# Half of a blocked fp32 projection through Strassen's seven products, on one Trainium2 core

## The chip, the cores and the metric

The kernel runs on one core of a Trainium2 chip. The metric is the device time of one execution in microseconds. Three runs of the kernel before gave a median of 1344.21 us (1343.96 to 1344.87).

## What is computed

A decoder block with 256 tokens and a model width of 2048: one combined input projection (2048 x 9216), attention and a gated MLP as token mixers, an output projection, a layer norm, and then the feed-forward part, which the change touches:

```
h = layer_norm(ALPHA * x + mix)
a = square(relu(h @ w_ff1 + b_ff1))      # 2048 -> 8192
y = layer_norm(ALPHA * h + a @ w_ff2 + b_ff2)   # 8192 -> 2048
```

Everything is fp32. The kernel splits every factor of a matrix product into a high part (the factor rounded to fp32r) and a low part (the rest), and adds the three products high x high, high x low and low x high.

## The kernel before

**Chunks, pieces, steps.** All weights pass through one pipeline. A chunk is 512 rows by 512 columns of a weight matrix (1 MB), loaded by SP's queue into one of three raw tiles (`issue_load`, L128). A piece is half a chunk: 256 rows, so two contraction tiles of 128 rows, by 512 columns. `emit_splits` (L152) takes a tile from a ring of six and makes the piece's high part on ScalarE (L171), and `emit_low` (L140) makes its low part on VectorE (L142). After the low part of a chunk's last piece the load of the third chunk after it is issued (L144). A step (`run_step`, L183) is TensorE's work with one piece; when it is done, the piece's tile goes back to the ring. So in step s the split of piece s + 5 is written into the program, and it waits until TensorE has finished step s - 1. The order of the steps is the order of the groups in the code, and each engine takes its instructions in the order in which the main loop (L766 to L780) writes them: the splits of the step, then deferred work (`rounds`, `later`), then the matmuls, then the evacuation of a group's accumulators.

**The feed-forward part** is cut into eight blocks of 1024 hidden columns. Block b has two groups of the first projection (`ff1`, 8 pieces each) and four groups of the last projection (`ff2`, one for each 512 output columns, 4 pieces each). The program runs the first projection of block b and then the last projection of block b - 1.

- A piece of `ff1` ("F" below) keeps the weights stationary: for each of 4 output tiles and 2 contraction tiles one matmul of 512 columns (the high weights times the high and low activations, L219) and one of 256 (the low weights times the high activations, L221). The four accumulators of the group come from a pool of six PSUM banks. Its evacuation is `halves` (L237): ScalarE copies one half of the bank with the bias (L242), VectorE adds the other (L244). Later steps square it (L535) and split it into high and low (`hilo`, L89 to L91).
- A piece of `ff2` ("E" below) keeps activations stationary: for each of 2 token tiles and 2 contraction tiles the three products of 512 columns (L207 to L209). The groups end with one addition of 128 x 512 per token tile into the residual y (L553).

**The end.** The last block's `ff2` groups run in an order by token tiles, with extra tiles (`LATE`, L544) beside the ring, and the second layer norm follows. Its gain and bias are loaded as wide tiles in blocks 2 and 3 (L703).

Of the kernel before, what the change touches and what calls it, by code (L numbers as in the profile page):

```python
# [11 lines left out]
F32 = mybir.dt.float32  # L12
F32R = mybir.dt.float32r
I32 = mybir.dt.int32
AF = mybir.ActivationFunctionType
ALU = mybir.AluOpType
AX = mybir.AxisListType

P = 128
S = 256  # L20
NT = S // P
# [7 lines left out]
CW = 512  # L29
# [3 lines left out]
RING = tuple(f"R{i}" for i in range(6))  # L33
LOOK = len(RING) - 1
NCT = CW // P
WARM = (256, 256, 256, 128)
EARLY = 3
NBUCKET = 32
# [30 lines left out]
def block_kernel(ctx: ExitStack, tc: tile.TileContext, xT, x, w_in, rel_bias, lnv_g, lnv_b, wsT, b_sp,  # L69
# [36 lines left out]
    def add_pieces(g, sizes=None, cs=None):  # L106
        out = []
        for c in cs or range(g.nk // KC):
            r0 = g.row + c * KC * P
            chunks.append(g.src[r0:r0 + KC * P, g.col:g.col + CW].rearrange("(k p) n -> p k n", p=P))  # L110
            k0 = 0
            for n in (sizes or {}).get(c, (KH,) * (KC // KH)):
                out.append(len(pieces))
                pieces.append(dict(g=g, chunk=len(chunks) - 1, k0=k0, k=c * KC + k0, n=n, last=k0 + n == KC, uses=0))
                k0 += n
        return out

    def add_step(piece, part, first=False, last=False):
        pieces[piece]["uses"] += 1
        steps.append((piece, part, first, last))  # L120
        return len(steps) - 1

    def add_group(g, sizes=None):
        hs = add_pieces(g, sizes)
        for h in hs:
            add_step(h, "all", h == hs[0], h == hs[-1])
# [10 lines left out]

    lows = []

    def emit_low(h):  # L140
        sl = raw_t[h["chunk"]][:, h["k0"]:h["k0"] + h["n"], :]
        nc.vector.tensor_tensor(h["lo"], sl, f32(h["hi"]), op=ALU.subtract)  # L142
        if h["last"]:
            issue_load(h["chunk"] + NRAW)  # L144
            for f in load_post.pop(h["chunk"], []):
                f()
# [5 lines left out]
    def emit_splits():  # L152


        while state["split"] < len(pieces):
            h = pieces[state["split"]]
            early = h["g"].early
            if lows and early is None:
                return
            tags = h["g"].tags  # L160
            tag = next((t for t in free if t in tags), None) or next((t for t in free if t in RING), None)
            if tag is None:
                return
            free.remove(tag)
            if h["chunk"] in split_with:
                split_with[h["chunk"]](h["k0"], h["n"])
            n = h["n"]
            t = big.tile([P, 2, KH, CW], F32R, name="w2", tag=tag)
            h["tag"], h["hi"], h["lo"] = tag, t[:, 0, :n, :], t[:, 1, :n, :]
            sl = raw_t[h["chunk"]][:, h["k0"]:h["k0"] + n, :]  # L170
            nc.scalar.activation(h["hi"], sl, AF.Copy)  # L171
            state["split"] += 1
            if early is not None and h["k"] >= early * KH:
                lows.append(h)
            else:
                emit_low(h)
# [6 lines left out]
    def run_step(s):  # L183
        piece, part, first, last = steps[s]
        h = pieces[piece]
        g, n, k0 = h["g"], h["n"], h["k"]
        hi, lo = h["hi"], h["lo"]
        if g.mode == "as":

            toks = range(NT) if part == "all" else [part]  # L190
            if n == 1:

                ps_ = [bank(g, i) for i in toks]
                av = g.act(k0)
                a = [[av[:, e * S + i * P:e * S + (i + 1) * P] for e in range(2)] for i in toks]
                for i in toks:
                    nc.tensor.matmul(ps_[i], a[i][0], hi[:, 0], start=first, stop=False)
                    nc.tensor.matmul(ps_[i], a[i][1], hi[:, 0], start=False, stop=False)
                for i in toks:
                    nc.tensor.matmul(ps_[i], a[i][0], lo[:, 0], start=False, stop=False)  # L200
            for i in toks if n > 1 else ():
                t, cs = (i[0], slice(i[1] * S, (i[1] + 1) * S)) if isinstance(i, tuple) else (i, slice(0, CW))
                p = bank(g, i)[:, cs]
                for kk in range(n):
                    av = g.act(k0 + kk)
                    ah, al = av[:, t * P:(t + 1) * P], av[:, S + t * P:S + (t + 1) * P]
                    nc.tensor.matmul(p, ah, hi[:, kk, cs], start=first and kk == 0, stop=False)  # L207
                    nc.tensor.matmul(p, ah, lo[:, kk, cs], start=False, stop=False)  # L208
                    nc.tensor.matmul(p, al, hi[:, kk, cs], start=False, stop=last and kk == n - 1)  # L209
        else:  # L210
            toks = {"lo01": (0, 1), "lo23": (2, 3)}.get(part, range(NCT))
            for ot in toks:
                p = bank(g, ot)
                ws_ = slice(ot * P, (ot + 1) * P)
                for kk in range(n):
                    av = g.act(k0 + kk)
                    st, en = first and kk == 0, last and kk == n - 1
                    if part == "all":
                        nc.tensor.matmul(p, hi[:, kk, ws_], av, start=st, stop=False)  # L219
                    if part in ("all", "lo01", "lo23"):  # L220
                        nc.tensor.matmul(p[:, :S], lo[:, kk, ws_], av[:, :S], start=False, stop=en)  # L221
                    if part in (0, 1):
                        ts = slice(part * P, (part + 1) * P)
                        nc.tensor.matmul(p.rearrange("p (a t) -> p a t", a=2)[:, :, ts], hi[:, kk, ws_],  # L224
                                         av.rearrange("p (a t) -> p a t", a=2)[:, :, ts], start=st, stop=False)
        h["uses"] -= 1
        if h["uses"] == 0:
            free.append(h["tag"])
        if last:
            for i in toks:  # L230
                g.evac(i, g.p.pop(i))
            if g.after and not g.p:
                g.after()

    later, rounds = [], []

    def halves(p, bias=None):  # L237
        t = work.tile([P, S], F32, name="half", tag="half", bufs=3)
# [276 lines left out]
    def load_wide(key, src, tag):  # L515
        tiles[key] = big.tile([P, D], F32, name="wide", tag=tag)
        nc.sync.dma_start(tiles[key], bcast(src, D))

    def residual2(c, part):
# [4 lines left out]
        else:  # L524
            y = tiles["y", part - 1][:, sl]
            nc.vector.scalar_tensor_tensor(y, y, ALPHA, tiles["ln1_g"][:, sl], op0=ALU.mult, op1=ALU.mult)
            nc.vector.tensor_tensor(y, y, bb, op=ALU.add)

    def ev_ff1(f):
        def fin(ot, s):  # L530
            if ot == 0:
                tiles["a", f] = big.tile([P, NCT, 2 * S], F32R, name="a", tag=f"A{f % 4}")
            a = tiles["a", f]
            q = work.tile([P, S], F32, name="sq", tag="sum", bufs=7)
            nc.vector.scalar_tensor_tensor(q, s, 0.0, s, op0=ALU.max, op1=ALU.mult)  # L535
            rounds.append((hilo, a[:, ot, :S], a[:, ot, S:], q))

        def ev(ot, p):
            k = f * NCT + ot
            later.append((fin, ot, halves(p, bff1[:, k:k + 1])))  # L540
        return ev

    NB = FF // 1024
    LATE = ("A4", "A5", "W", "S10", "S11", "S12")  # L544

    def ev_ff2(blk, c):
        def ev(i, p):
# [67 lines left out]
    def quad(key):  # L615
        return lambda k: tiles[key][k // 4][:, k % 4, :]
# [5 lines left out]
    def at(s, f, *a):  # L622
        side.setdefault(s, []).append((f, a))
# [55 lines left out]
    for part in (0, 1, "lo01", "lo23"):  # L679
        for h in hs:  # L680
            s = add_step(h, part, part == 0 and h == hs[0], part not in (0, 1) and h == hs[-1])

    def ff1(f):
        add_group(Group(w_ff1, f * CW, 16, quad("hT"), "ws", ev_ff1(f), tags=wide if f == 1 else ()))

    def ff2(blk, c):
        return Group(w_ff2, c * CW, 8, lambda k: tiles["a", 2 * blk + k // NCT][:, k % NCT, :], "as",
                     ev_ff2(blk, c), row=blk * 1024, tags=LATE if blk == NB - 1 else ())

# [4 lines left out]
            at(s + 13 + 3 * i + j, residual2, i, j)  # L694
    for b in range(1, NB):
        j = len(chunks)
        ff1(2 * b)
        ff1(2 * b + 1)
        if b == 1:
            for i, a in enumerate((("ln1_b", ln1_b, "S11"), ("b_ff2", b_ff2, "S10"), ("ln1_g", ln1_g, "S12"))):  # L700
                load_post[j + 2 * i] = [lambda a=a: load_wide(*a)]
        elif b < 4:
            load_post[j] = [lambda a=(("ln2_b", ln2_b, "S6"), ("ln2_g", ln2_g, "S13"))[b - 2]: load_wide(*a)]  # L703
        if b == NB - 1:
            at(len(steps), free.extend, LATE[:3])
        for c in range(4):
            add_group(ff2(b - 1, c))
    add_group(ff2(NB - 1, 0))
    hss = [add_pieces(ff2(NB - 1, c)) for c in range(1, 4)]
    for part, hs in ((0, hss[0]), (0, hss[1]), (0, hss[2]), (1, hss[0]), (1, hss[1]), ((1, 0), hss[2]), ((1, 1), hss[2])):  # L710
# [104 lines left out]
```

## Time and profile before

| | |
|---|---|
| median of 3 runs | 1344.21 us |
| the profiled execution | 1344.47 us, of which its span is 1342.8 us |
| TensorE matmuls busy | 1331.8 us, 99% of the span, 6916 matmuls |
| VectorE busy | 831.7 us, 62% |
| ScalarE busy | 625.8 us, 47% |
| GpSimd busy | 5.1 us |
| DMA | 259.46 MB, 193 GB/s |

The profile is of one execution. The span goes from its first to its last instruction. Busy times are sums over an engine's instructions without overlaps. Matmuls overlap in the array, so a matmul's own duration is longer than the distance to the next one: it is the distance that counts for the time.

### The profile page before, as it was taken

The numbers are of one execution on the slowest core, as the hardware profiler recorded it, in microseconds if no ns is written. First come the engines' busy times: TensorE is split into PE (matmuls) and PEld (weight loads), VectorE is DVE, ScalarE is ACT, GpSimd is POOL, SyncE is SP. The second block draws the span as 40 slices with busy tenths as digits, with TensorE's granted clock in tenths as the row PEclk, the third lists the DMA queues.
The fourth block names the chain that finished last, engine by engine and source line by source line (L and its number), as shares of the span: only waits on it lengthen the run. The fifth ranks groups of instructions, "written<-read, shape, count | busy, mean of one in ns | idle before, by whom it ended". The sixth has DMA issues, their size and how long they took to land.

```text
span 1342.8 us, 17128 instructions
## 1 busy us (share of the span) xinstructions
PE 1331.8 (99%) x6916; PEld 1126.9 (84%) x6916; DVE 831.7 (62%) x1183; ACT 625.8 (47%) x832; POOL 5.1 (0%) x15
## 2 busy tenths in 40 slices
PE   8999999999999999999999999999999999999997
PEld 6888888888888888889888888888888888888886
DVE  6554677564545787568669565565565655655666
ACT  4444465454545555345554443443544434435531
POOL 0000000000000000000000000000000000000000
PEclk9999999999999999999999999999999999999999
DMA  9766445555555567553865656656555555565541
GB/s 324 277 193 218 158 157 169 181 183 189 188 189 187 176 199 254 180 196 116 287 224 188 219 188 213 194 184 187 189 185 190 188 183 190 184 186 190 187 174 63
DMA packets 128800, 259.46 MB, mean 193 GB/s; under 512 B 4808, under 2 KB 7376, under 8 KB 127824
## 3 DMA queue, kind: packets, MB, share of 16 engines
q1 hardware_dynamic: 127984, 254.94, 57.9%
q0 software_dynamic: 592, 3.16, 0.7%
q8 instruction: 54, 0.88, 0.3%
q10 hardware_dynamic: 144, 0.26, 0.1%
q14 instruction: 26, 0.21, 0.0%
HBM read 256.23 MB, written 2.11 MB: 192 GB/s over the span
## 4 chain that ended last, share of the span: by engine, by line
PE 97%; DMA 1%; DVE 1%; ACT 0%; issue 0%; SPq 0%; DVEq 0%
PE mm L219 36%; PE mm L221 19%; PE mm L208 13%; PE mm L209 13%; PE mm L207 13%; PE mm L224 1%; DVE w L142 1%; DMA raw<-in_w_in_dram 1%; DMA raw<-in_w_ff_dram 0%; DMA xraw<-in_xT_dram 0%; PE aux L387 0%; PE aux L495 0%; PE aux L295 0%; PE aux L325 0%; PE aux L317 0%
## 5 line engine op out<-in xcount | busy, mean ns | idle before, releaser
L142 DVE TENSOR_TENSOR w<-raw,w 128x1024 fp32r<-128x1024 f32 (+1 forms) x466 | 565.6, 1219 | 459.4 <-ACT w L171 459.3
L171 ACT ACTIVATE w<-raw 128x1024 fp32r<-128x1024 f32 (+1 forms) x466 | 489.6, 1055 | 603.3 <-PE mm L221 335.6
L219 PE MATMUL mm<-hT,w 128*128 128x512 f32 x960 | 336.6, 393 | 0.8 <-DVE sum L244 0.8
L219 PE MATMUL mm<-xs,w 128*128 128x512 f32 x896 | 315.7, 395 | 0.0
L221 PE MATMUL mm<-hT,w 128*128 128x256 f32 x1024 | 275.7, 279 | 0.0
L221 PE MATMUL mm<-xs,w 128*128 128x256 f32 x896 | 250.0, 279 | 0.0
L219 PEld LDWEIGHTS mm<-hT,w 128*128 128x128 f32 x960 | 179.9, 187 | 44.0 <-DVE sum L244 1.1
L209 PE MATMUL mm<-w,a 128*128 128x512 f32 (+1 forms) x520 | 204.1, 392 | 0.0
L207 PE MATMUL mm<-w,a 128*128 128x512 f32 (+1 forms) x520 | 204.1, 392 | 0.0
L208 PE MATMUL mm<-w,a 128*128 128x512 f32 (+1 forms) x520 | 204.1, 392 | 0.0
L219 PEld LDWEIGHTS mm<-xs,w 128*128 128x128 f32 x896 | 167.9, 187 | 39.7
L221 PEld LDWEIGHTS mm<-hT,w 128*128 128x128 f32 x1024 | 187.7, 188 | 0.3
L221 PEld LDWEIGHTS mm<-xs,w 128*128 128x128 f32 x896 | 168.0, 187 | 0.2
L207 PEld LDWEIGHTS mm<-w,a 128*128 128x128 f32 x520 | 97.9, 188 | 23.0
L209 PEld LDWEIGHTS mm<-w,a 128*128 128x128 f32 x520 | 97.9, 188 | 22.9
L208 PEld LDWEIGHTS mm<-w,a 128*128 128x128 f32 x520 | 97.9, 188 | 22.7
L207 PE MATMUL mm<-w,merged 128*128 128x512 f32 x128 | 50.9, 398 | 0.0
L209 PE MATMUL mm<-w,merged 128*128 128x512 f32 x128 | 50.7, 396 | 0.0
L208 PE MATMUL mm<-w,merged 128*128 128x512 f32 x128 | 50.7, 396 | 0.0
L207 PE MATMUL mm<-w,xs 128*128 128x512 f32 x120 | 49.5, 412 | 1.0 <-ACT w L171 1.0
L244 DVE TENSOR_TENSOR sum<-mm,half 128x256 f32<-128x256 f32 x136 | 49.0, 417 | 0.0
L208 PE MATMUL mm<-w,xs 128*128 128x512 f32 x120 | 47.7, 397 | 1.3 <-DVE w L142 1.3
(142 smaller groups left out, 970.7 us busy)
## 6 DMA issues: line engine op xcount, KB each, us to landing
raw<-in_w_ff_dram SPq DMA_DIRECT2D x128, 1024.0 KB, 5.2
raw<-in_w_in_dram SPq DMA_DIRECT2D x68, 1024.0 KB, 5.1
raw<-in_w_out_dram SPq DMA_DIRECT2D x16, 1024.0 KB, 5.1
raw<-in_w_pa_dram SPq DMA_DIRECT2D x8, 1024.0 KB, 5.1
raw<-in_w_pb_dram SPq DMA_DIRECT2D x8, 1024.0 KB, 5.1
raw<-in_w_in_dram SPq DMA_DIRECT2D x6, 512.0 KB, 8.0
y<-in_x_dram POOLq DMA_DIRECT2D x2, 1024.0 KB, 6.3
wide<-in_ln_b_dram SPq DMA_DIRECT2D x2, 1024.0 KB, 8.4
```

The lines of the kernel that those rows point to most:

```text
L142: nc.vector.tensor_tensor(h["lo"], sl, f32(h["hi"]), op=ALU.subtract)
L171: nc.scalar.activation(h["hi"], sl, AF.Copy)
L207: nc.tensor.matmul(p, ah, hi[:, kk, cs], start=first and kk == 0, stop=False)
L208: nc.tensor.matmul(p, ah, lo[:, kk, cs], start=False, stop=False)
L209: nc.tensor.matmul(p, al, hi[:, kk, cs], start=False, stop=last and kk == n - 1)
L219: nc.tensor.matmul(p, hi[:, kk, ws_], av, start=st, stop=False)
L221: nc.tensor.matmul(p[:, :S], lo[:, kk, ws_], av[:, :S], start=False, stop=en)
L224: nc.tensor.matmul(p.rearrange("p (a t) -> p a t", a=2)[:, :, ts], hi[:, kk, ws_], av.rearrange("p (a t) -> p a t", a=2)[:, :, ts], start= ...
L244: nc.vector.tensor_tensor(s, p[:, :S], t, op=ALU.add)
```

## The change

In blocks 1 to 6 the output columns 0 to 1023 of the last projection are no longer computed as 8 products of (128 tokens x 512) times (512 x 512), but as 7 (Strassen's scheme; the code names them P1 to P7). The columns 1024 to 2047 stay as they were.

- **Weights.** P3 and P2 use a chunk of the weights as it is and go through the raw tiles. The five others take their weights from two held tiles of 1 MB (tags S10 and S11). GpSimd's queue loads them, and adds further weight blocks to them by DMAs with `accum_op=add`. Tile 0 is used by P1, then one block is added, P5, another block, P6, a third block, P4. Tile 1 is a load and an addition, for P7. So each block has two plain loads and four adding ones on GpSimd's queue. An addition is issued after the low part of the last piece that used the tile's former value.
- **Activations.** VectorE makes four sums of 128 x 128 for each of four column tiles (`sum_of_acts`), and ScalarE and VectorE split them into high and low, after the second `ff1` group of a block.
- **Steps.** A piece of a product is used for one 128-token tile only: 6 matmuls of 512 columns. Products accumulate in the two banks of the small PSUM pool. P1, P5, P6 and P7 are added up over the six blocks in a tile `acc` (in the first block copied there by ScalarE), P3, P2 and P4 in y. At the end `collect` combines them with 8 additions of 128 x 512.
- **Order.** The 38 steps of a section follow `ORDER`: 16 F of the next block, 14 pieces of products and 8 E. `mixed` writes it out, for sections 2 to 7.
- The wide loads of the second layer norm's gain and bias move to the start of the last block's `ff2`, and so do the extra tiles of `LATE`.

```diff
+ORDER = ("F F F P1 F P1 F F F P5 F P5 F F F P6 F P6 F P3 P3 F P7 F P7 F "
+         "E P2 E P2 E E P4 E P4 E E E").split()
...
+    def add_held(g, key, done=None):
+        out = []
+        for k0 in range(0, KC, KH):
+            out.append(len(pieces))
+            pieces.append(dict(g=g, chunk=None, held=key, done=done, k0=k0, k=k0, n=KH, last=k0 + KH == KC, uses=0))
+        return out
...
+    def source(h):
+        t = tiles[h["held"]] if h["chunk"] is None else raw_t[h["chunk"]]
+        return t[:, h["k0"]:h["k0"] + h["n"], :]
     def emit_low(h):
-        sl = raw_t[h["chunk"]][:, h["k0"]:h["k0"] + h["n"], :]
+        sl = source(h)
         nc.vector.tensor_tensor(h["lo"], sl, f32(h["hi"]), op=ALU.subtract)
-        if h["last"]:
+        if h["last"] and h["chunk"] is None:
+            if h["done"]:
+                h["done"]()
+        elif h["last"]:
             issue_load(h["chunk"] + NRAW)
             for f in load_post.pop(h["chunk"], []):
                 f()
...
-            sl = raw_t[h["chunk"]][:, h["k0"]:h["k0"] + n, :]
-            nc.scalar.activation(h["hi"], sl, AF.Copy)
+            nc.scalar.activation(h["hi"], source(h), AF.Copy)
...
+        if g.mode == "sum":
+            if first:
+                sums["p"] = psx.tile([P, CW], F32, name="aux")
+            p = sums["p"]
+            for kk in range(n):
+                ah, al = g.act(k0 + kk)
+                nc.tensor.matmul(p, ah, hi[:, kk], start=first and kk == 0, stop=False)
+                nc.tensor.matmul(p, ah, lo[:, kk], start=False, stop=False)
+                nc.tensor.matmul(p, al, hi[:, kk], start=False, stop=last and kk == n - 1)
+            h["uses"] -= 1
+            if h["uses"] == 0:
+                free.append(h["tag"])
+            if last:
+                g.evac(p)
+            return
...
+    later, rounds, sums = [], [], {}
...
+    def sum_of_acts(f, ot, q):
+        if f % 2 == 0:
+            return
+        if ot == 0:
+            for i in range(2):
+                tiles["ca", i] = big.tile([P, 2, NCT, 2, P], F32R, name="ca", tag=("S6", "S13")[i])
+        q0, t0, t1 = tiles["q", ot], slice(0, P), slice(P, S)
+        cb = work.tile([P, 4, P], F32, name="cb", tag="pt")
+        nc.vector.tensor_tensor(cb[:, 0], q0[:, t1], q[:, t1], op=ALU.subtract)
+        nc.vector.tensor_tensor(cb[:, 2], q0[:, t0], q0[:, t1], op=ALU.subtract)
+        nc.vector.tensor_tensor(cb[:, 1], cb[:, 0], q0[:, t0], op=ALU.subtract)
+        nc.vector.tensor_tensor(cb[:, 3], q[:, t0], cb[:, 1], op=ALU.add)
+        for i in range(2):
+            d = tiles["ca", i][:, :, ot]
+            rounds.append((hilo, d[:, :, 0], d[:, :, 1], cb[:, 2 * i:2 * i + 2]))
...
+            summed = f // 2 in SUMMED
+            if summed and f % 2 == 0:
+                q = tiles["q", ot] = work.tile([P, S], F32, name="q0", tag="es"[ot // 2])
+            else:
+                q = work.tile([P, S], F32, name="sq", tag="sum", bufs=7)
             nc.vector.scalar_tensor_tensor(q, s, 0.0, s, op0=ALU.max, op1=ALU.mult)
             rounds.append((hilo, a[:, ot, :S], a[:, ot, S:], q))
+            if summed:
+                sum_of_acts(f, ot, q)
...
-    LATE = ("A4", "A5", "W", "S10", "S11", "S12")
+    SUMMED = range(1, NB - 1)
+    def held_load(blk, i):
+        def block(r, c):
+            r0 = blk * 1024 + r * CW
+            return w_ff2[r0:r0 + CW, c * CW:(c + 1) * CW].rearrange("(k p) n -> p k n", p=P)
+        tiles["b", i] = big.tile([P, KC, CW], F32, name="held", tag=("S10", "S11")[i])
+        nc.gpsimd.dma_start(tiles["b", i], block(0, i))
+        if i == 1:
+            nc.gpsimd.dma_start(tiles["b", 1], block(1, 1), accum_op=ALU.add)
+    def held_add(blk, r, c):
+        def f():
+            r0 = blk * 1024 + r * CW
+            nc.gpsimd.dma_start(tiles["b", 0], w_ff2[r0:r0 + CW, c * CW:(c + 1) * CW]
+                                .rearrange("(k p) n -> p k n", p=P), accum_op=ALU.add)
+        return f
...
+    def products(blk):
...
+        def plain(r, t):
+            def f(k):
+                v = tiles["a", 2 * blk + r][:, k, :]
+                return v[:, t * P:(t + 1) * P], v[:, S + t * P:S + (t + 1) * P]
+            return f
+        def summed(i):
+            def f(k):
+                v = tiles["ca", i // 2][:, i % 2, k]
+                return v[:, 0], v[:, 1]
+            return f
+        def ev(into):
+            def f(p):
+                if isinstance(into, tuple):
+                    d = tiles["y", into[0]][:, into[1] * CW:(into[1] + 1) * CW]
+                else:
+                    if ("acc", into) not in tiles:
+                        if "acc" not in tiles:
+                            tiles["acc"] = big.tile([P, 4, CW], F32, name="acc", tag="S12")
+                        d = tiles["acc", into] = tiles["acc"][:, into]
+                        nc.scalar.activation(d, p, AF.Copy)
+                        return
+                    d = tiles["acc", into]
+                nc.vector.tensor_tensor(d, d, p, op=ALU.add)
+            return f
+        more = blk + 1 in SUMMED
+        out = {}
+        for name, act, b, done, into in (
+                ("P1", plain(0, 0), 0, held_add(blk, 0, 1), 0),
+                ("P5", summed(0), 0, held_add(blk, 1, 1), 1),
+                ("P6", summed(1), 0, held_add(blk, 1, 0), 2),
+                ("P3", summed(3), (1, 1), None, (0, 1)),
+                ("P7", summed(2), 1, (lambda: held_load(blk + 1, 1)) if more else None, 3),
+                ("P2", plain(1, 0), (1, 0), None, (0, 0)),
+                ("P4", plain(1, 1), 0, (lambda: held_load(blk + 1, 0)) if more else None, (1, 0))):
+            if isinstance(b, int):
+                g = Group(None, 0, KC, act, "sum", ev(into))
+                out[name] = lambda g=g, b=b, done=done: add_held(g, ("b", b), done)
+            else:
+                g = Group(w_ff2, b[1] * CW, KC, act, "sum", ev(into), row=blk * 1024 + b[0] * CW)
+                out[name] = lambda g=g: add_pieces(g)
+        return out
+    def collect(i):
+        y = [[tiles["y", t][:, c * CW:(c + 1) * CW] for c in range(2)] for t in range(NT)]
+        p1, p5, p6, p7 = (tiles["acc"][:, k] for k in range(4))
+        d, a, b, op = ((y[0][0], y[0][0], p1, ALU.add), (y[0][1], y[0][1], p5, ALU.add), (p1, p1, p6, ALU.add),
+                       (y[0][1], y[0][1], p1, ALU.subtract), (p7, p7, p1, ALU.add), (y[1][0], y[1][0], p7, ALU.add),
+                       (y[1][1], y[1][1], p5, ALU.add), (y[1][1], y[1][1], p7, ALU.subtract))[i]
+        nc.vector.tensor_tensor(d, a, b, op=op)
+    def mixed(b):
+        made = {"F": [ff1_group(2 * b), ff1_group(2 * b + 1)], "E": [ff2(b - 1, c) for c in (2, 3)]}
+        prods = products(b - 1)
+        if b - 1 == SUMMED[0]:
+            for i in range(2):
+                at(len(steps) - 7, held_load, b - 1, i)
+        left = {}
+        queue = {"F": [], "E": []}
+        for name in ORDER:
+            if name in prods:
+                if name not in left:
+                    hs = prods[name]()
+                    left[name] = [(h, h == hs[0], h == hs[-1]) for h in hs]
+                q = left[name]
+            else:
+                q = queue[name]
+                if not q:
+                    g = made[name].pop(0)
+                    for c in range(g.nk // KC):
+                        q.append((g, c, None))
+                if q[0][2] is None:
+                    g, c, _ = q.pop(0)
+                    hs = add_pieces(g, None, (c,))
+                    q[:0] = [(h, c == 0 and h == hs[0], c == g.nk // KC - 1 and h == hs[-1]) for h in hs]
+            h, f, l = q.pop(0)
+            add_step(h, "all", f, l)
+    LATE = ("A4", "A5", "W", "S5", "S10", "S11")
...
+    def ff1_group(f):
+        return Group(w_ff1, f * CW, 16, quad("hT"), "ws", ev_ff1(f))
...
+        if b - 1 in SUMMED:
+            mixed(b)
+            continue
...
-        elif b < 4:
-            load_post[j] = [lambda a=(("ln2_b", ln2_b, "S6"), ("ln2_g", ln2_g, "S13"))[b - 2]: load_wide(*a)]
-        if b == NB - 1:
-            at(len(steps), free.extend, LATE[:3])
         for c in range(4):
             add_group(ff2(b - 1, c))
+    at(len(steps), free.extend, LATE[:4])
+    for i, a in enumerate((("ln2_b", ln2_b, "S6"), ("ln2_g", ln2_g, "S13"))):
+        load_post[len(chunks) + i] = [lambda a=a: load_wide(*a)]
+    for i in range(8):
+        at(len(steps) + i // 2, collect, i)
```

## Rows read from the trace of the kernel before

**Rows 1.** The page, busy time: engine, busy us, share of the span, instructions
```profile
PE 1331.8 (99%) x6916; PEld 1126.9 (84%) x6916; DVE 831.7 (62%) x1183; ACT 625.8 (47%) x832; POOL 5.1 (0%) x15
```

**Rows 2.** The page, chain that ended last, by engine
```profile
PE 97%; DMA 1%; DVE 1%; ACT 0%; issue 0%; SPq 0%; DVEq 0%
```

**Rows 3.** Waits of TensorE: engine, line, waited for, us, times, longest
```profile
PE aux L607 <- ACT dg L603: 2.0, 1, 2.0
PE mm L208 <- DVE w L142: 1.3, 2, 0.8
...
PE mm L219 <- DVE sum L244: 0.8, 1, 0.8
```

**Rows 4.** Windows of three sections: us, busy by engine (instructions), clock, DMA share, GB/s
```profile
706.00:795.80 89.80, 89.80 (x450) 75.20 (x449) 61.63 (x81) 39.77 (x48) 0.00 (x0) 1.00 0.61 199
...
885.60:975.40 89.80, 89.80 (x450) 75.20 (x449) 52.08 (x66) 39.65 (x48) 0.00 (x0) 1.00 0.59 187
1155.00:1244.80 89.80, 89.80 (x450) 75.26 (x449) 52.08 (x65) 39.65 (x48) 0.00 (x0) 1.00 0.59 188
```

**Rows 5.** Timeline of TensorE: start us, duration, instruction; first F, first and 97th E
```profile
699.68 0.39 PE L219 MATMUL mm<-hT,w 128*128 128x512 f32 x1
...
703.18 0.40 PE L207 MATMUL mm<-w,a 128*128 128x512 f32 x1
...
725.67 0.40 PE L207 MATMUL mm<-w,a 128*128 128x512 f32 x1
```

**Rows 6.** Groups by form: busy us, mean ns | idle before
```profile
L142 DVE TENSOR_TENSOR w<-raw,w 128x1024 fp32r<-128x1024 f32 x462 | 562.8, 1224 | 459.4 <-ACT w L171 459.3
...
L242 ACT ACTIVATE half<-mm,bff 128x256 f32<-128x256 f32 x64 | 29.2, 470 | 6.7 <-PE mm L221 6.7
...
L305 DVE SCALAR_TENSOR_TENSOR s<-e,mult 128x128 f32<-128x128 f32 x8 | 2.3, 282 | 0.0
```

**Rows 7.** Timeline of VectorE, instructions that follow without a gap
```profile
780.26 1.23 DVE L142 TENSOR_TENSOR w<-raw,w 128x1024 fp32r<-128x1024 f32 x1 [0.90 <-ACT w L171]
781.40 0.42 DVE L91 TENSOR_TENSOR a<-sq,a 128x256 fp32r<-128x256 f32 x1
781.73 0.42 DVE L535 SCALAR_TENSOR_TENSOR sq<-sum 128x256 f32<-128x256 f32 x1
...
1253.44 1.28 DVE L553 TENSOR_TENSOR y<-y,mm 128x512 f32<-128x512 f32 x2
```

**Rows 8.** Timeline of ScalarE, two instructions without a gap
```profile
779.16 1.06 ACT L171 ACTIVATE w<-raw 128x1024 fp32r<-128x1024 f32 x1 [1.44 <-PE mm L221]
780.13 0.40 ACT L90 ACTIVATE a<-sq 128x256 fp32r<-128x256 f32 x1
```

**Rows 9.** DMA issues: count, KB each, median us from issue to landing
```profile
raw<-in_w_ff_dram SPq DMA_DIRECT2D x128, 1024.0 KB, 5.2
...
y<-in_x_dram POOLq DMA_DIRECT2D x2, 1024.0 KB, 6.3
```

**Rows 10.** The tile y, 500 to 530 us: GpSimd's two loads, issue to landing
```profile
DMA to landing us min/median/max: 5.3/6.3/7.3
```

**Rows 11.** DMA queue of SP: packets, MB, share of 16 engines' span
```profile
q1 hardware_dynamic: 127984, 254.94, 57.9%
```

**Rows 12.** Timeline of GpSimd: the issues of its two 1 MB loads
```profile
513.49 0.55 POOL L464 DMA_DIRECT2D y<-in_x_dram  x1 [388.28 <-PE mm L221]
519.03 0.54 POOL L464 DMA_DIRECT2D y<-in_x_dram  x1 [5.00 <-DVE sum L244]
```

**Rows 13.** Window of the stretch with GpSimd's two loads, columns as in rows 4
```profile
510.00:530.00 20.00, 20.00 (x100) 16.77 (x99) 16.15 (x27) 10.03 (x16) 1.09 (x2) 1.00 0.82 292
```

More of the change, by code (lines that the diff above doesn't have):

```diff
@@ L233, in run_step @@
                 g.after()
-    later, rounds = [], []
+    later, rounds, sums = [], [], {}
     def halves(p, bias=None):
@@ L533, in fin @@
             a = tiles["a", f]
-            q = work.tile([P, S], F32, name="sq", tag="sum", bufs=7)
+            summed = f // 2 in SUMMED
[3 more added lines that the diff above has]
+                q = work.tile([P, S], F32, name="sq", tag="sum", bufs=7)
             nc.vector.scalar_tensor_tensor(q, s, 0.0, s, op0=ALU.max, op1=ALU.mult)
             rounds.append((hilo, a[:, ot, :S], a[:, ot, S:], q))
+            if summed:
+                sum_of_acts(f, ot, q)
         def ev(ot, p):
```

## Prediction

> **What bounds the kernel now.** I read the busy times first: TensorE is busy 99% of the span, VectorE 62%, ScalarE 47% [rows 1]. Busy matmuls overlap, so the chain of waits comes next: 97% of the way to the last instruction is TensorE itself [rows 2]. Then TensorE's waits: the largest is one of 2.0 us near the end of the kernel, those for a low part or a sum come to 1.3 and 0.8 us in all [rows 3]. The windows show the stretch that is changed: each section of 32 steps takes 89.8 us at a granted clock of 1.00 (the 2.4 GHz level), with VectorE busy 52.1 us, ScalarE 39.7, the DMA engines 0.59 [rows 4]. So the time of a section is the number of its matmuls times their distance. Matmuls of 512 columns in an E follow each other in (725.67 - 703.18) / 96 = 0.234 us, and a pair of 512 and 256 columns in an F in (703.18 - 699.68) / 10 = 0.350 us [rows 5]. An F has 8 pairs, 2.80 us; an E 12 matmuls, 2.81 us; 16 of each are 89.8 us, which the window has.
>
> **What is removed.** Half of a section's E work is 8 products of 12 matmuls, 96; seven are 84. The 12 left out are 12 x 0.2343 = 2.81 us per section, in six sections 16.9 us. A piece of a product now has 6 matmuls, 1.41 us, so a section is 16 x 2.80 + 8 x 2.81 + 14 x 1.41 = 87.0 us.
>
> **What is added on VectorE and ScalarE.** Fourteen product pieces stand where 8 E pieces stood: 6 more low parts at 1.22 us on VectorE [rows 6] and as many high parts at 1.06 on ScalarE [rows 8]. The sums of activations are 16 instructions of 128x128, 0.28 us each [rows 6], and 8 further splits at 0.42 on VectorE [rows 7] and 0.40 on ScalarE [rows 8]; 7 evacuations replace 4, at 0.68 (1.28 for two that overlap [rows 7]). VectorE: 52.1 + 7.3 + 4.5 + 3.4 + 2.0 = 69.3 of 87.0 us, 80%. ScalarE: 39.7 + 6.4 + 3.2 = 49.3, 57%. Neither fills the section, and TensorE's lead of five steps hides them if no stretch is crowded. The worst one begins where the second F group ends (step 25): four steps then carry a square, four sums, and one step later three low parts, beside the piece's own. Without a gap instructions follow faster than their durations: 1.14 us after a low part, 0.33 after 256 columns, 0.6 after 512 [rows 7]; for 128 columns I estimate 0.2, as 0.28 less the same 0.08. From the end of step 25, the low part of step 35's piece is done after 1.5 + 5 x 1.14 + 4 x (0.33 + 0.8) + 9 x 0.33 + 0.6 = 15.3 us (with full durations 18.4); step 35 begins at 2.81 x 6 + 1.41 x 2 = 19.7 us. Cost nothing; the cover is TensorE's lead, 4.4 us of it.
>
> **What is added on queues.** GpSimd's queue gets six 1 MB DMAs per section, four of them adding. An issue took it 0.55 us [rows 12]. Queue order matters little: the addition to tile 1 waits on GpSimd for its plain load, some 6 us, and behind it stands only the load for the next P1, which has over 10 us. SP loads 14 chunks per section instead of 16, so nothing more is queued there. The loads of gain and bias move to the end, where the LATE tiles give TensorE a lead; the eight additions of `collect` (8 x 0.6 us [rows 7]) fall into four steps of 11.2 us that also hold four low parts (4.6): nothing for either.
>
> **What is added as waits: the adding DMAs.** P5's weights exist when an addition has landed, and ScalarE, which takes its work in order, stops in front of their split. Take time 0 at a section's start. The low part of P1's second piece (step 5) can be split then; behind E's two evacuations it is done at 2.7, and the first addition is issued. Call its time to landing A1. P5's first piece (step 9) can be split from 9.8 on, when step 3 ends. After it follow the splits of steps 10 and 11 and P1's evacuation: 1.0 + 3 x 1.14 + 0.6, with hand-overs 5.2. So P5's second low part is done at 7.9 + A1, or at 16.9 if the addition is early, and the second addition (A2) is issued, for P6's piece (step 15). That split is written in step 10 ahead of the evacuation of the first F group (`halves`). The second F group starts at 28.0 (step 12); of six PSUM banks two are free, so its third output tile, at 29.4, needs the first bank back: split 1.0, half 0.47 [rows 6], sum 0.42 (256 columns [rows 7]). The second addition must have landed at 27.4. Hence **A2 up to 10.5 us and A1 + A2 up to 19.5 us** cost nothing; what exceeds this stops TensorE in each section. At an excess of 2.81 us (11.2 us for each) the gain is gone.
>
> No adding DMA is in the trace. From below, a plain 1 MB load from GpSimd's queue took 6.3 us in the middle [rows 9], 5.3 and 7.3 for its two [rows 10]: if reading the tile costs nothing, no stall. From above, two such in series, 12.6: an excess of 25.2 - 19.5 = 5.7 us. I take the lower end plus the data a second time, since both addends pass the engines while issue and completion come once. A packet of SP's queue held an engine 0.579 x 16 x 1342.8 / 127984 = 0.097 us [rows 11]; 1 MB is 512 rows of 2 KB, 32 per engine, 3.1 us. So A1 = 5.3 + 3.1 = 8.4 (only one raw load falls late into it) and A2 = 7.3 + 3.1 = 10.4 (two do). The sum, 18.8, leaves 0.7; A2 alone leaves 0.1, so I put 0.2 us per section, 1.2 in all.
>
> The Trainium skill (Collectives: The Full Stack, section on the bandwidth ceiling) has a price for such an add: the unit reads two sources through one ring, at a rate 1.93 times lower; as an estimate from this the data take 6.0 us, both additions 18.4, and the time would be 1327.6 us. No run here shows it yet.
>
> The profiled execution took 1344.47 us. Less 16.9, plus 1.2: 1328.8. That execution is 0.26 us above the median 1344.21, so I predict 1328.5 us.
>
> **Rivals.**
>
> *The additions are slower than their cover: slower than before.* If an adding DMA passes its data three times (read, read, write one after another), it takes 6.3 + 2 x 3.1 = 12.5 us, with an excess of 5.5 us per section at the third output tile of step 12; 33 - 16.9 = 16 us lost, 1360 us. The DMA engines say the same: 16 loads took 0.59 x 89.8 = 53 us of a section [rows 4], 3.3 each; four additions at 6.6 make 79 of 87 us, at 9.9 they make 92.4, more than the old 89.8, and the raw loads would be late too. It decides from 11.2 us per addition. For it speaks the crowded 91%; against it, that GpSimd's two loads took 6.3 us at a DMA share of 0.82 [rows 13]. Chance 0.25.
>
> *GpSimd's issues stand behind VectorE.* If every issue waits for one low part (1.23 us), both additions grow by 1.2: 21.2, an excess of 1.7 us, 1338 us. Against it: with VectorE busy 16.15 of 20 us, GpSimd's two issues took 0.55 and 0.54 us [rows 12, 13]. This is what the Trainium skill (SBUF — State Buffer, section on who interferes with whom) would make of VectorE instructions with two SBUF inputs beside a reading GpSimd. The trace does not bear it out for plain loads. With this go all cases in which additions take 9.9 to 10.9 us. Chance 0.23.
>
> *Gain and stalls balance*: additions of 11 to 11.4 us give 1344 us, not to be told from no change. Chance 0.1.
>
> That seven products do not save their matmuls can't be: the count is in the code, and L207's distance does not depend on where the activations lie.
>
> **How the numbers follow.** The forecast has 0.42 (below 1331). A measurement here can tell 0.2%, 2.7 us, from no change. Faster by more: 0.42 + 0.23 = 0.65; the same 0.1; slower 0.25. The range goes from 1326 (full gain, no stall, and the spread of the runs) to 1362 (the upper bound of 12.6 per addition, 1344.2 - 16.9 + 34.2), since slower cases up to there are needed to leave out no more than 2 in 10. The faster cases by themselves lie between 1326 and 1341.
>
> **What would show it.** Right: sections of 87 us, 6844 matmuls, VectorE near 69 us per section, adding DMAs landing in 8 to 10.5 us, and no wait of TensorE for the sum of `halves` in step 12. Wrong: TensorE waiting there or for a low part in each of six sections, with the addition as the releaser of ScalarE's split; or DMA shares near 1. If sections are 87 us and the time is not down, the loss lies in the last block.

## The result and the profile after

The changed kernel took 1328.63 us (median of 4 runs, 1327.70 to 1329.04), the kernel before in the same comparison 1344.54 us: a ratio of 0.9881 with a 95% interval of 0.9869 to 0.9893. The forecast was 1328.5 us.

The page of the changed kernel: busy times, GpSimd's DMA queue (packets, MB, share of 16 engines' span), and the line for GpSimd's loads (count, KB each, median us from issue to landing; 24 of the 36 are additions):

```profile
span 1326.9 us, 17376 instructions
PE 1315.2 (99%) x6844; PEld 1112.9 (84%) x6844; DVE 919.6 (69%) x1385; ACT 680.9 (51%) x920; POOL 45.0 (3%) x51
...
q0 software_dynamic: 16528, 40.91, 14.3%
...
held<-in_w_ff_dram POOLq DMA_DIRECT2D x36, 1024.0 KB, 8.4
```

TensorE still bounds the kernel, with 72 matmuls less than in [rows 1]. Of its waits (what was waited for, us in all, times, longest) one group in the changed sections is new, that of L212:

```profile
PE aux L768 <- ACT dg L764: 2.0, 1, 2.0
...
PE aux L212 <- DVE w L156: 1.1, 2, 0.8
PE mm L251 <- DVE sum L276: 0.7, 1, 0.7
```

L212 is a matmul of a product: TensorE waited twice, 1.1 us in all, for the low part of a product's weights. Both waits are in the first changed section, at P5's first piece (step 9, at 770.96) and P6's (step 15, at 786.00). From start to start these two steps take 1.97 and 2.44 us there and 1.39 in the third section, together 1.6 us more. The windows of the first three changed sections (columns as in [rows 4]):

```profile
747.80:836.40 88.60, 87.53 (x438) 73.00 (x437) 62.79 (x93) 49.24 (x66) 7.96 (x7) 1.00 0.88 258
836.40:923.30 86.90, 86.90 (x438) 72.95 (x436) 66.95 (x99) 48.70 (x62) 6.64 (x6) 1.00 0.85 246
923.30:1010.20 86.90, 86.90 (x437) 72.98 (x436) 66.36 (x98) 48.71 (x62) 6.64 (x6) 1.00 0.84 243
```

From the second section on, TensorE is busy without a gap. From each first F to the next, sections 2 to 5 take 86.92 us and the first 88.56. Against the 89.8 us of [rows 4], with the sixth taken as the second, that is 5 x 2.88 + 1.24 = 15.6 us; the spans differ by 1342.8 - 1326.9 = 15.9. VectorE has 66.4 us of work in a section, ScalarE 48.7, and the DMA engines' share is 0.84 to 0.88.

The timeline of GpSimd shows the DMAs of the first section and of the third (L609 a plain load, L611 the addition to tile 1, L616 an addition to tile 0):

```profile
737.92 1.52 POOL L609 DMA_DIRECT2D held<-in_w_ff_dram  x2 [218.46 <-DVE y L559]
748.66 1.31 POOL L611 DMA_DIRECT2D held<-in_w_ff_dram  x1 [9.22 <-DMA held<-in_w_ff_dram]
750.63 1.29 POOL L616 DMA_DIRECT2D held<-in_w_ff_dram  x1 [0.66 <-DVE w L156]
772.62 1.26 POOL L616 DMA_DIRECT2D held<-in_w_ff_dram  x1 [20.70 <-DVE w L156]
...
926.18 1.26 POOL L616 DMA_DIRECT2D held<-in_w_ff_dram  x1 [20.68 <-DVE w L156]
940.45 1.26 POOL L616 DMA_DIRECT2D held<-in_w_ff_dram  x1 [13.01 <-DVE w L156]
955.23 1.30 POOL L616 DMA_DIRECT2D held<-in_w_ff_dram  x1 [13.52 <-DVE w L156]
```

The third section starts at 923.30. Its first addition is issued 2.9 us later, the second 17.2, as the prediction had it (2.7 and 16.9). The trace's rows for the tile `held`, each for the window around one issue, give the time to landing: 8.3 us for the one at 926.18 and 8.3 for the one at 940.45. In the first section it is 17.9 us for the issue at 750.63, which stands 2 us behind the addition to tile 1, and 11.0 for the one at 772.62:

```profile
DMA to landing us min/median/max: 8.3/8.3/8.3
...
DMA to landing us min/median/max: 17.9/17.9/17.9
```

ScalarE's timeline shows what the second addition meets. First the third section, then the first:

```profile
948.26 0.92 ACT L274 ACTIVATE half<-mm,bff 128x256 f32<-128x256 f32 x2
...
950.48 2.08 ACT L187 ACTIVATE w<-held 128x1024 fp32r<-128x1024 f32 x2
...
777.30 0.47 ACT L274 ACTIVATE half<-mm,bff 128x256 f32<-128x256 f32 x1 [1.34 <-DVE sum L276]
783.62 1.06 ACT L187 ACTIVATE w<-held 128x1024 fp32r<-128x1024 f32 x1 [5.85 <-DMA held<-in_w_ff_dram]
```

The evacuation of the F group (L274) stands *ahead* of the split of P6's weights (`w<-held` at 950.48 and 783.62). The prediction had it behind. The reason is in the code: `emit_splits` goes through the list of pieces, not through the steps. A chunk's two pieces stand next to each other in the list, even if a product's piece lies between them among the steps, and so P6's first piece is written one step later, after the evacuation. The second addition is then needed only for step 15 itself, which starts 36.4 us into a section. Between its landing and the start of the matmul that needs the low part lie 2.4 us (783.62 to 786.00 in the first section).

So three theories were open. *On record*: additions over 10.5 us (the second) or 19.5 us (both) stop TensorE at step 12. *List order*: the second may land up to 36.4 - 17.2 - 2.4 = 16.8 us after its issue, and both together may take 28.9 - 1.6 = 27.3 us (the first section's sum less its loss); TensorE then waits at step 15. The first addition by itself may take 17.9 - 0.6 = 17.3 us by it, since step 9 lost 0.6 us. *Something else*: the additions cost by crowding the DMA engines, or the gain is not the matmuls.

### The profile page after: what moved, and what is told of

It reads as the page before. It is cut to its first block, busy times and chain, and to the rows that moved or that the text cites. A ratio compares the mean times of both kernels' runs of the same rounds, so it can differ in the third digit from the quotient of the medians.

```text
span 1326.9 us, 17376 instructions
## 1 busy us (share of the span) xinstructions
PE 1315.2 (99%) x6844; PEld 1112.9 (84%) x6844; DVE 919.6 (69%) x1385; ACT 680.9 (51%) x920; POOL 45.0 (3%) x51
## 3 DMA queue, kind: packets, MB, share of 16 engines
q0 software_dynamic: 16528, 40.91, 14.3%
## 5 line engine op out<-in xcount | busy, mean ns | idle before, releaser
L156 DVE TENSOR_TENSOR w<-raw,w 128x1024 fp32r<-128x1024 f32 (+1 forms) x442 | 533.7, 1217 | 324.0 <-ACT w L187 323.2
L187 ACT ACTIVATE w<-raw 128x1024 fp32r<-128x1024 f32 (+1 forms) x442 | 461.1, 1053 | 437.8 <-PE mm L253 300.4
L241 PE MATMUL mm<-w,a 128*128 128x512 f32 (+1 forms) x328 | 128.1, 390 | 0.0
L240 PE MATMUL mm<-w,a 128*128 128x512 f32 (+1 forms) x328 | 128.0, 390 | 0.0
L239 PE MATMUL mm<-w,a 128*128 128x512 f32 (+1 forms) x328 | 127.8, 390 | 0.0
L156 DVE TENSOR_TENSOR w<-held,w 128x1024 fp32r<-128x1024 f32 x60 | 73.3, 1221 | 38.2 <-ACT w L187 37.8
L187 ACT ACTIVATE w<-held 128x1024 fp32r<-128x1024 f32 x60 | 63.3, 1058 | 59.7 <-PE mm L241 23.4
L239 PEld LDWEIGHTS mm<-w,a 128*128 128x128 f32 x328 | 61.8, 188 | 14.3
L241 PEld LDWEIGHTS mm<-w,a 128*128 128x128 f32 x328 | 61.7, 188 | 14.0
L240 PEld LDWEIGHTS mm<-w,a 128*128 128x128 f32 x328 | 61.8, 188 | 13.9
L239 PE MATMUL mm<-w,xs 128*128 128x512 f32 x120 | 49.5, 412 | 0.5 <-ACT w L187 0.5
```

The lines of the kernel that those rows point to most:

```text
L187: nc.scalar.activation(h["hi"], source(h), AF.Copy)
```

## Experiments

**The load of tile 1 later in the first section** (`late_tile1`; the next kernels but the two that follow and the last build on it):

```diff
-            for i in range(2):
-                at(len(steps) - 7, held_load, b - 1, i)
+            at(len(steps) - 7, held_load, b - 1, 0)
+            at(len(steps) + 7, held_load, b - 1, 1)
```

> Only the first section is changed: tile 1 is loaded and added to 7 steps into it instead of 7 steps ahead of it, so the first addition to tile 0 no longer shares the DMA engines with it. If that sharing made the first addition land after 17.9 us and so cost the 1.6 us by which the first section is longer than the others (88.6 against 86.9), the time falls by 1.6 us against the changed kernel, to about 1327.0, with all sections at 86.9. Rival: the first section is longer because ScalarE copies four products into acc there; then nothing changes (1328.6). By the limit on record (second addition up to 10.5 us) the second addition, which now shares, would stop TensorE by 1 us or more in this section, 1328.

Measured: 1327.35 us (1326.69 to 1327.70, 4 runs), a ratio of 0.9875 (0.9859 to 0.9892) to the kernel before. The sections take 86.93 us (the first) and 86.92. The waits of TensorE no longer hold a product's matmul:

```profile
PE aux L768 <- ACT dg L764: 2.0, 1, 2.0
PE mm L240 <- DVE w L156: 1.3, 2, 0.8
PE aux L918 <- POOL vb L915: 1.2, 1, 1.2
PE mm L251 <- DVE sum L276: 0.8, 1, 0.8
```

The first section's loss of 1.6 us is gone, and ScalarE still copies the four products into `acc` there: it came from the addition to tile 1 just ahead on the same queue and the same DMA engines. Which of the two made the landing late, no run tells apart. In the medians the loss is 1.3 us, and the intervals of the two ratios overlap, so the section's length is the better evidence. The second addition, now the one beside the load of tile 1, landed after 9.0 us, under the limit on record too, so this run doesn't test that limit. The kernel computes the same as the changed one and was the shortest of all that were run.

**Plain loads for the additions** (on the changed kernel; the sums of weights are left out, one block stands for each):

```diff
-            nc.gpsimd.dma_start(tiles["b", 1], block(1, 1), accum_op=ALU.add)
+            nc.gpsimd.dma_start(tiles["b", 1], block(1, 1))
...
-                                .rearrange("(k p) n -> p k n", p=P), accum_op=ALU.add)
+                                .rearrange("(k p) n -> p k n", p=P))
```

> Every adding DMA becomes a plain load of the same bytes, so the products take one block of weights where a sum should stand (the sums of weights are left out). If the additions are wholly covered, as the trace shows in sections 2 to 6, landing falls from 8.4 to about 5.5 us and the time only by the first section's stall: 1327 to 1328.6. Rival, that the additions cost TensorE something by crowding the DMA engines: the time falls by 3 us or more.

Measured: 1327.71 us (1327.46 to 1327.95, 4 runs), ratio 0.9877 (0.9862 to 0.9892). All five sections that can be measured are 86.92 or 86.93 us long. GpSimd's queue and the issues of this kernel's DMAs:

```profile
q0 software_dynamic: 10384, 40.91, 8.9%
...
held<-in_w_ff_dram POOLq DMA_DIRECT2D x36, 1024.0 KB, 5.6
```

Landing takes 5.6 us (the median of all 36) instead of 8.4, and the sections are as long as with additions. Where an addition is covered it costs TensorE nothing, also not by the DMA engines' higher share (0.84 and 0.85 in the second and third section, 0.74 and 0.73 here). The queue's rows show what an addition moves: 14.3% of 1326.9 us less 8.9% of 1326.2 are 72 us for each of the 16 engines, so 3.0 us for each of the 24 additions, one more pass of 1 MB (3.1 us in the prediction) and not two.

**Eight products' matmuls** (on the changed kernel; P4 counts twice):

```diff
+            again = getattr(g, "again", 1)
-            for kk in range(n):
+            for kk in range(n * again):
...
+                g.again = 2 if name == "P4" else 1
```

> P4's matmuls are issued twice, so a section has 12 matmuls more, as many as without Strassen, and everything else of the change stays (P4 counts twice). If the gain is the matmuls and nothing else, 6 x 2.81 = 16.9 us come back: 1345.5. Rival, that part of the gain came from the order or from the end of the kernel: clearly below 1343.

Measured: 1345.67 us (1345.04 to 1346.41, 10 runs). The sections take 89.73 us (the first 91.15), 2.81 more. With the old number of matmuls and everything else of the change, the time is the old one and the first section's loss: ratio 1.0011 (1.0002 to 1.0020). The gain is the matmuls, all of it.

**The second addition twice** (on `late_tile1`; its block counts twice in P6 and P4):

```diff
+            for _ in range(2 if (r, c) == (1, 1) else 1):
-            nc.gpsimd.dma_start(tiles["b", 0], w_ff2[r0:r0 + CW, c * CW:(c + 1) * CW]
-                                .rearrange("(k p) n -> p k n", p=P), accum_op=ALU.add)
+                nc.gpsimd.dma_start(tiles["b", 0], w_ff2[r0:r0 + CW, c * CW:(c + 1) * CW]
+                                    .rearrange("(k p) n -> p k n", p=P), accum_op=ALU.add)
```

> On late_tile1; the second addition of each section is made twice, one after the other, so that A2 is some 17 us instead of 8.4 and A1 stays 8.4 (its block of weights counts twice in P6 and P4). By the limits on record (A2 up to 10.5 us, A1 + A2 up to 19.5, since P6's split was thought to stand ahead of the evacuation of the first F group) the excess is 6.5 us per section, 39 us in all: 1366. By the order that the trace of the changed kernel shows (splits follow the list of pieces, in which P6's come one step later, behind that evacuation) P6's low part is needed only at the start of step 15, 36.4 us into the section: an addition issued at 17.2 may take 16.8 us, so 0.2 us per section, 1327 to 1330.

Measured: 1362.63 us (1361.62 to 1365.65, 4 runs), 35.3 us above `late_tile1`. By its size alone this looks like the 39 us that the limits on record give. But the two additions took longer than assumed. Timeline of GpSimd, and the start of ScalarE's split behind them:

```profile
953.58 1.28 POOL L617 DMA_DIRECT2D held<-in_w_ff_dram  x1 [12.51 <-DVE w L156]
962.57 1.27 POOL L617 DMA_DIRECT2D held<-in_w_ff_dram  x1 [7.71 <-DMA held<-in_w_ff_dram]
```
```profile
973.92 2.00 ACT L187 ACTIVATE w<-held 128x1024 fp32r<-128x1024 f32 x2 [10.28 <-DMA held<-in_w_ff_dram]
```

A2 was 973.9 - 953.6 = 20.3 us. By the limits on record this is 9.8 us too much, at step 12, and 59 us in all; by the list order 20.3 - 16.8 = 3.5 us, at step 15. TensorE's timeline in that section, from the last F of step 14 (the section starts at 936.36, so step 15 is due at 972.76):

```profile
972.65 0.28 PE L253 MATMUL mm<-hT,w 128*128 128x256 f32 x1
975.03 0.49 PE L211 MATMUL aux<-w,ca 128*128 128x512 f32 x1 [2.10 <-ACT w L187]
976.29 0.50 PE L212 MATMUL aux<-w,ca 128*128 128x512 f32 x1 [0.77 <-DVE w L156]
...
978.14 0.63 PE L251 MATMUL mm<-hT,w 128*128 128x512 f32 x1
978.57 0.41 PE L253 MATMUL mm<-hT,w 128*128 128x256 f32 x1
978.78 0.63 PE L251 MATMUL mm<-hT,w 128*128 128x512 f32 x1
```

The three F of steps 12 to 14 ran without a stop; TensorE waited 2.10 + 0.77 = 2.9 us at step 15, in the other sections 2.7 to 4.4. (These count from the modelled end of the matmul before; from start to start the two stops put TensorE off by 2.25 + 1.03 = 3.3 us.) The list order holds, the limit on record falls. The rest of the loss stands in the rows behind the wait: 512 and 256 columns then take 0.43 and 0.21 us, the level of 1.2 GHz, instead of 0.23 and 0.12. The windows before, during and after:

```profile
968.00:972.00 4.00, 4.00 (x25) 3.46 (x24) 0.00 (x0) 0.00 (x0) 0.00 (x0) 1.00 1.12 205
...
975.00:978.00 3.00, 2.20 (x6) 1.61 (x7) 2.99 (x4) 2.29 (x3) 0.00 (x0) 0.81 0.00 0
978.00:982.00 4.00, 4.00 (x18) 3.38 (x18) 4.00 (x8) 2.55 (x4) 1.27 (x1) 0.72 0.28 31
982.00:986.00 4.00, 4.00 (x22) 3.41 (x22) 4.00 (x6) 3.45 (x5) 0.00 (x0) 1.00 1.10 206
```

P6's first piece took 3.11 us instead of 1.40, of which the stop was 1.03, and the F behind it 3.80 instead of 2.80: 0.7 + 1.0 = 1.7 us lost at the lower clock. With the 3.3 us of stops this is the 5.0 us by which the section is longer. The sections take 91.7 to 94.3 us, 4.8 to 7.4 more than in `late_tile1`.

**Both additions twice** (on `late_tile1`; as above, for all c == 1):

> On late_tile1; the first and the second addition are each made twice (both blocks count twice where they are added), A1 and A2 some 17 us each. By the limits on record the excess is 34 - 19.5 = 14.5 us per section, 87 us: 1414. By the order in the trace the limit for A1 + A2 is 27.3 us (the first section of the changed kernel had 17.9 + 11.0 = 28.9 us and stopped TensorE for 1.6): 34 - 27.3 = 6.7 us per section, 40 us: 1367, with TensorE waiting at P6's first piece.

Measured: 1426.73 us (1423.84 to 1428.53, 4 runs), 99.4 above `late_tile1`. TensorE's waits of this kernel are all at products, none at an F, and the granted clock is lower after them:

```profile
PE aux L211 <- ACT w L187: 57.4, 12, 7.3
PE aux L212 <- DVE w L156: 7.1, 12, 0.8
```
```profile
986.00:1003.00 17.00, 11.82 (x64) 9.98 (x62) 3.83 (x7) 1.46 (x4) 1.26 (x1) 0.90 1.04 247
1003.00:1009.00 6.00, 3.41 (x7) 2.43 (x8) 3.90 (x7) 3.37 (x4) 0.25 (x1) 0.50 0.02 3
```

The waits come to 64.5 us, 10.8 per section, twice in each (at P5's and P6's first piece). The profiled execution's span is 97.1 us longer than that of `late_tile1`; the other 33 us are not idle time. In the section of these windows the clock is below 1 behind both stops, and the mean granted clock of the run is 0.97 instead of 1.00. Here too the pairs took longer than 17 us: in one section the four additions landed 8.3, 11.9, 9.2 and 10.2 us after their issues, and from the first issue of a pair to the landing of its second it was 20.7 and 19.7 us. By the list order, 20.7 - 17.3 = 3.4 us of delay were due at P5, and 40.4 - 27.3 = 13.1 in all; by the limits on record 40.4 - 19.5 = 20.9. In that section TensorE was put off by 3.4 us at P5 and 8.5 at P6, from start to start, and by 1.6 at the lower clock between them: 13.5. The measured time lies above both numbers of the expectation (1367 and 1414) and bears out neither; the place and the size of the delays bear out the list order.

**Sums of activations three times** (on `late_tile1`, same values):

```diff
+        for _ in range(3):
-        nc.vector.tensor_tensor(cb[:, 0], q0[:, t1], q[:, t1], op=ALU.subtract)
+            nc.vector.tensor_tensor(cb[:, 0], q0[:, t1], q[:, t1], op=ALU.subtract)
...
```

> On late_tile1; the four sums of activations are made three times in a row (same values), so that VectorE has 8 x 0.21 = 1.7 us more in each of the four steps behind the second F group, up to 6.6 us at the low part of step 35's piece. In the trace of the changed kernel this low part is done 2.8 us before TensorE needs it: then 3.8 us are lost in each of the five sections in which the sums fall among product pieces, 19 us, 1346. By the lead of 4.4 us on record 2.2 us per section, 1338. If VectorE had room for it, as its 76% of a section suggest, nothing is lost.

Measured: 1355.93 us (1355.54 to 1357.05, 4 runs), 28.6 more. A changed section takes 91.5 us, 4.6 more, and in it TensorE waits for low parts at two E pieces:

```profile
1013.46 0.50 PE L240 MATMUL mm<-w,a 128*128 128x512 f32 x1 [2.54 <-DVE w L156]
...
1019.45 0.50 PE L240 MATMUL mm<-w,a 128*128 128x512 f32 x1 [1.52 <-DVE w L156]
```
```profile
1013.00:1016.00 3.00, 2.54 (x11) 2.09 (x12) 2.93 (x11) 1.09 (x2) 0.00 (x0) 1.00 0.09 37
```

From start to start the two stops are 2.8 + 1.8 = 4.6 us, the whole loss of the section: here the granted clock stays at 1.00.

Five sections make 23 us. The other 5 or 6 stand in front of them: the first changed section starts at 753.1 instead of 747.3, as block 1 has the sums too, which the expectation had thought covered. VectorE's lead behind the second F group is there, and it is short: 6.6 us more work were 4.6 too many. By the lead of 2.8 us in the trace it would have been 3.8; the other 0.8 is not explained.

**All products in one stretch** (on the changed kernel):

```diff
-ORDER = ("F F F P1 F P1 F F F P5 F P5 F F F P6 F P6 F P3 P3 F P7 F P7 F "
-         "E P2 E P2 E E P4 E P4 E E E").split()
+ORDER = ("P1 P1 P5 P5 P6 P6 P3 P3 P7 P7 P2 P2 P4 P4 " + "F " * 16 + "E " * 8).split()
```

> ORDER with all 14 product pieces in one stretch at the section's start, then 16 F, then 8 E. Nothing stands between P5 and P6 but a second addition: 8.4 us to landing, one high part and one low part, less TensorE's work in between; I expect a wait of about 8 us at P6 and about 1 us at P4 in each section: 6 x 9 = 54 us more, about 1383. If TensorE's lead of five pieces hid the additions wherever they stand, it would stay near 1329.

Measured: 1457.73 us in one run, 129 more; sections of 106 to 119 us instead of 86.9, more than twice the loss expected. TensorE's longest wait in one of them, and VectorE around it:

```profile
995.66 0.77 PE L210 MATMUL aux<-w,ca 128*128 128x512 f32 x1 [12.03 <-DVE acc L646]
```
```profile
990.22 1.23 DVE L155 TENSOR_TENSOR w<-held,w 128x1024 fp32r<-128x1024 f32 x1 [9.87 <-ACT w L186]
991.36 1.28 DVE L713 TENSOR_TENSOR y<-y,mm 128x512 f32<-128x512 f32 x2
992.56 1.22 DVE L155 TENSOR_TENSOR w<-held,w 128x1024 fp32r<-128x1024 f32 x1
993.70 1.22 DVE L155 TENSOR_TENSOR w<-raw,w 128x1024 fp32r<-128x1024 f32 x1
994.83 0.68 DVE L646 TENSOR_TENSOR acc<-acc,aux 128x512 f32<-128x512 f32 x1
```

TensorE stands from 983.63. Until 990.2 P6's weights are not split, which is the wait for the addition that was expected (6.6 us). P6's first low part is done at 991.4, but TensorE starts only at 995.66. From 990.2 on it waits for a PSUM bank: two serve the products, and P1's evacuation (L646) stands on VectorE behind that low part, two evacuations of E and two further low parts. My expectation had left this out. In all, TensorE's waits at products come to 102 us of the 129; most of the rest goes with the lower clock (a mean of 0.96 over this run, 1.00 in the changed kernel).

## Why the prediction was right

- **What is removed: right.** 72 matmuls less; sections of 86.92 us against 87.0 forecast. With 12 matmuls put back the sections are 2.81 us longer and the gain is gone: shown.
- **VectorE and ScalarE: right.** 66.4 us per section on VectorE (69.3 forecast: durations were added that overlap) and 48.7 on ScalarE (49.3). The lead behind the second F group was forecast as 4.4 us. In the trace the low part of step 35's piece (the line below) is done at 997.78 + 1.22 = 999.0, 16.9 us after the end of step 25 against 15.3 forecast, and the step starts at 1001.79: 2.8 us. The term was too favourable by 1.6 us, still on the safe side, and the kernel with the sums three times shows that it ends there.

```profile
997.78 1.22 DVE L156 TENSOR_TENSOR w<-raw,w 128x1024 fp32r<-128x1024 f32 x1
```

- **The price of an addition: right for the first, too high for the second.** From the second section on the two took 8.3 to 9.8 us, mostly 8.3 or 8.4. That is the 8.4 forecast for the first; the second stayed at 8.3 to 9.2 against 10.4, so what was added to it for two raw loads did not come. The choice (a plain load and the data once more) held: 8.4 against 5.6 for a plain load is 2.8 us for the second pass, 3.1 forecast, and the queue's rows give 3.0. The Trainium skill (Collectives: The Full Stack, section on the bandwidth ceiling) has a rate 1.93 times below a copy's for the adding step of a collective, which reads two sources; with 3.1 us of data that is an estimate of 2.9 more for these DMAs, and these traces agree.
- **The cover: wrong in its working.** The limits of 10.5 and 19.5 us came from taking the splits in the order of the steps. They follow the list of pieces, so that the halves stand ahead of P6's split, and TensorE waits at step 15, when the second addition takes more than 16.8 us. The doubled second addition shows it: no stop at step 12, 2.9 us at step 15. From the second section on nothing came of the error only because the additions lay under both limits. The first section shows it too: with 17.9 + 11.0 = 28.9 us a stop of 9.4 us was due at step 12 by the limit of 19.5, and 1.6 us came, at steps 9 and 15.
- **The 1.2 us put down for stalls: right in size, wrong in place.** No section lost 0.2 us. The first lost 1.6, since there the addition to tile 1 and the first addition to tile 0 are issued 2 us apart and share one queue and the engines (17.9 us to landing). The prediction had not looked at the first section by itself and had put queue order down as of little matter. Moving one load by 14 steps takes this away. That 1.6 us stand where 1.2 were put down is luck, and with it a part of the nearness of 1328.63 to 1328.5.
- **Rivals.** Additions of 11 us or more did not come in the regular sections. At 0.85 the DMA engines stayed below the 91% forecast. GpSimd's issues did not stand behind VectorE: those of additions took 1.26 to 1.31 us in every section, whether VectorE was idle or busy. The windows of two issues in the changed kernel, with VectorE (third busy time) at 0.00 and at 1.30 us:

```profile
750.63:751.92 1.29, 1.29 (x9) 1.14 (x8) 0.00 (x0) 1.06 (x1) 1.28 (x1) 1.00 1.05 387
955.23:956.53 1.30, 1.30 (x9) 1.12 (x8) 1.30 (x2) 0.56 (x2) 1.29 (x1) 1.00 0.00 0
```

- **Two slips without effect.** With full durations the sum for step 35 is 18.2 us, not 18.4. And 1327.6 us, the prediction's time by the rate 1.93 times lower, is that of the profiled execution; less 0.26 it is 1327.3.

## What to carry to other kernels

Arithmetic that is saved on the bounding engine pays in full if what makes up for it (summing, extra splits, transfers) lies on other engines and its deadlines are met; so the work of the estimate is the deadlines, not the totals. Take the order of each engine's instructions from the loop that writes them, here a list that differs from the order of the steps by one place, and treat the first round apart, where transfers that are spread later on start together. A missed deadline can cost more than its wait: stops of 3.3 us on TensorE cost 1.7 us more by the clock in one run, stops of 2.8 and 1.8 us nothing more in another.

## What the runs showed of the hardware that was not expected

- An adding DMA of 1 MB occupied GpSimd for 1.26 to 1.31 us, a plain one of the same shape 0.76 to 0.79, and the plain loads of [rows 12], which have longer rows, 0.55.
- Two additions to one tile in a row take more than twice 8.4 us: the second is issued when the first has landed, and landed 11.3 to 12.4 us after its issue with the second addition doubled, 8.9 to 11.9 with both. Why it is slower stays open.
- After a wait of 2.9 us TensorE's granted clock was 0.81 and 0.72 in the next 3 and 4 us, with matmuls of 512 columns 0.43 us apart, and 1.7 us were lost by it. With the sums three times a single wait of 2.54 us left it at 1.00, and so did the shorter waits in the first section of the changed kernel.
